# Chunk-output stage: states copied for two groups at once, kernel products ordered by kind, two copies turned into loads

## The chip, the cores and the metric

The kernel runs on one core of a Trainium2 chip. The metric is the time of one execution on the device in microseconds (us). Four such times of the kernel before are known: 2605.39, 2610.87 and 2609.28 us (median 2609.28), and 2605.47 us for the execution that was profiled.

## The reference

A model of two layers over 2048 latent tokens of 1024 channels, with a context of 256 tokens. Layer 0 is windowed attention; the change doesn't touch it. Layer 1 is a bidirectional state-space layer with 64 groups of 16 channels and 64 complex states per group and direction:

```python
for dirn in range(2):
    a_bar = exp(lam * dt)                       # one complex number per group and state
    b_bar = ((a_bar - 1.0) / lam)[..., None] * b_mat
    bu = einsum('gph,blgh->blgp', b_bar, ug)    # ug: inputs of the layer, by group
    xs = diag_scan(a_bar, bu)                   # x[t] = a_bar * x[t-1] + bu[t], started from the context's last state
    y = y + einsum('ghp,blgp->blgh', c_mat, xs).real
y = y + d * ug                                  # then gelu, a GLU and an output projection
```

All inputs and the output are float32.

## The kernel before, in words

The kernel is one program of stages: attention, the input projection of layer 1 (u), chunk states, the scan over chunks, the projection z, the chunk outputs, the GLU, and the output projection. Time is cut into 128 chunks of 16 tokens. For each group, the output of a chunk is the sum of two matrix products: "own" (the chunk's own 256 inputs times a 256 x 256 matrix of kernel values) and "state" (the state that enters the chunk, real and imaginary part, both directions, times a table of powers times C).

The scan leaves the states in one big tile `sall`, as 144 chunk positions x real and imaginary x 64 groups, 128 partitions (64 states of each direction). So the states of one group over the chunks stand 512 bytes apart.

The chunk outputs are made by `phase5` in 16 steps `q` of four groups each. A step's order is written out in a string, for most steps `S0 S1 T2 K T2 G N O0 L O1 L B2 B3` (P5P):

- `S0`, `S1`: for group 0 and 1 of the step `state_part` copies that group's states out of `sall` into a tile `xT` (two activations on ACT, lines 1717 and 1719, one for each direction), and `state_mm` (line 1724) multiplies: `xT` is the stationary operand (the weights), the table `gr` or `gi` the moving one.
- `K`: `ker` makes the kernel values of the next step: for each direction and group a 64-column product (line 1688), for each group a 16-column product with `cb` (line 1693), and one product that adds the skip term to the diagonal (line 1687). They go into one PSUM tile, are copied to `ks` by ACT (line 1697), written to DRAM `qqd` in four pieces (line 1699), and loaded back as the matrices `mq` of the next step's own products (`load_m`, line 1708; two at the end of K, two at the `L`).
- `G`: `gen` makes `gr` and `gi` of the step after the next on POOL (line 1598) and DVE (1599, 1600) from a table tile `tab5`, which `load_tab` (1568) fetches from DRAM `tabd`; the first of their 17 columns is a plain copy of C by ACT (line 1582).
- `N`: `prep` makes the operands `bm` (POOL 1615, DVE 1616 and 1619), `g4` (ACT 1676, from `gr` and `gi`) and `cb` (ACT 1671, a copy out of the table) for the kernel products of the step after the next.
- `O0`, `O1`: own products (line 1735) of groups 0 and 1; `B2`, `B3`: own and state products of groups 2 and 3. A Gelu on ACT (line 1792) follows each group.
- `T2`: two flips back into token order, each of four transposes of 128 x 128 (line 1749) and one copy (line 1753); four flips follow every second step.

Step 0 and the last step have strings of their own (P50, P5L). What stands in the strings is the program's order of writing; a planner then sets the order of each engine's instructions from a simulated timeline, except that the kinds of instructions that `keep` marks (own products, kernel products, and on ACT the copies of lines 1582, 1671, 1676 and 1697) stay in the order of writing. The engines, and the queue of SP, which issues all DMAs of this stage, each work strictly in that planned order.

A float32 matrix product is two passes on TensorE, each with a weight load (PEld) of its own; the profile counts the passes.

Of the kernel before, what the change touches and what calls it, by code (L numbers as in the profile page):

```python
# [6 lines left out]
F32 = mybir.dt.float32  # L7
# [3 lines left out]
AF = mybir.ActivationFunctionType  # L11
# [14 lines left out]
def dap(t, offset, dims):  # L26
    return bass.AP(tensor=t.tensor, offset=t.offset + offset, ap=[list(d) for d in dims])
# [31 lines left out]
WUS = [(2, 'vg'), (1, 'v'), (1, 'v')]  # L59
CS = -2  # L60
RS = 50
MB = 6
ZE = (1, 4, 0)
ZG = 1
ZW = 'vv'
# [21 lines left out]
class Net:  # L87
# [1468 lines left out]
    def phase5(self, uy, sall, es):  # L1556
        nc, a, net = self.nc, self.a, self
        el = ExitStack()
        ps = el.enter_context(self.pool("p5ps", 2, PSUM))
        G, M, pools = {}, {}, []  # L1560
# [4 lines left out]
        def load_tab(q):  # L1565
            sl, hf = divmod(q, 2)
            tab = pools[0].tile([128, 7, 4, 16], F32, name=f"tab5{q % 2}")
            nc.sync.dma_start(tab, self.tabd[sl, :, 2:9].rearrange("p j (g h) -> p j g h", g=8)[:, :, hf * 4:hf * 4 + 4])
            return tab

        def gen(q, tab=None):
            tab = tab or load_tab(q)

            def pw(j):
                return tab[:, 2 + j, :, :, None].to_broadcast([128, 4, 16, 16])

            def cc(j):
                return tab[:, 4 + j, :, None, :].to_broadcast([128, 4, 16, 16])

            gr, gi = (pools[0 if q % 3 == 1 else 2].tile([128, 4, 17, 16], F32, name=f"g{n}{q % 3}") for n in "ri")  # L1580
            for t, j in ((gr, 4), (gi, 5)):
                self.keep("E", nc.scalar.activation(t[:, :, 0], tab[:, j], AF.Copy))
            grw, giw = gr[:, :, 1:17], gi[:, :, 1:17]
            for w, j, k, op in ((grw, 1, 0, OP.add), (giw, 0, 1, OP.subtract)):
                if q < 2:
                    nc.gpsimd.tensor_tensor(w, pw(0), cc(k), op=OP.mult)
                    for h in range(0, 4, 2):
                        hs = slice(h, h + 2)
                        m = ps.tile([128, 4, 128], F32, name="ytp").rearrange("p a b -> p (a b)")
                        m = m.rearrange("p (g t h) -> p g t h", g=2, t=16)  # L1590
                        ins = nc.vector.tensor_mul(m, pw(1)[:, hs], cc(j)[:, hs])
                        if j and h == 0:
                            self.keep("Z", ins)
                        nc.vector.tensor_tensor(w[:, hs], w[:, hs], m, op=op)
                else:
                    m = pools[2].tile([128, 4, 16, 16], F32, name="gm") if j else free[:, 448:1472].rearrange(
                        "p (g t h) -> p g t h", g=4, t=16)
                    nc.gpsimd.tensor_tensor(m, pw(1), cc(j), op=OP.mult)
                    nc.vector.tensor_mul(w, pw(0), cc(k))
                    nc.vector.tensor_tensor(w, w, m, op=op)  # L1600
            G[q] = (gr, gi, tab)
# [4 lines left out]
        def kernel_parts(q, tab, bm, kts, kd, dk):  # L1606
            nc.vector.tensor_mul(kd, self.ident[0:16, None, 0:16].to_broadcast([16, 4, 16]),
                                 dk[:, :, None].to_broadcast([16, 4, 16]))
            mt = ps.tile([128, 2, 256], F32, name="bmt", bufs=1)
            for ri, op in enumerate((OP.subtract, OP.add)):  # L1610
                pr, pi = (tab[:, 6, :, r * 4:r * 4 + 4, None].to_broadcast([128, 4, 4, 16]) for r in range(2))
                br, bi = (tab[:, r, :, None, :].to_broadcast([128, 4, 4, 16]) for r in (ri, 1 - ri))
                kt = kts[ri].rearrange("p (g a) h -> p g a h", a=4)
                m = mt[:, ri].rearrange("p (g a h) -> p g a h", g=4, a=4)
                nc.gpsimd.tensor_tensor(kt, pr, br, op=OP.mult)
                nc.vector.tensor_mul(m, pi, bi)
                for d in range(2):
                    hs = slice(d * 64, (d + 1) * 64)
                    nc.vector.tensor_tensor(bm[ri * 64:(ri + 1) * 64, 1 - d], kt[hs], m[hs], op=op)
# [4 lines left out]
        def first():  # L1624
# [30 lines left out]
            for _ in ker(0):  # L1655
                pass
# [4 lines left out]
        def prep(q):  # L1661
            tab = G[q][2]
            kts = [free[:, c:c + 256].rearrange("p (r h) -> p r h", h=16) for c in (0, 1472)]
            kd = free[0:16, 256 + q % 2 * 64:320 + q % 2 * 64].rearrange("p (g h) -> p g h", h=16)
            bm = pools[1].tile([128, 2, 4, 4, 16], F32, name="bm")
            kernel_parts(q, tab, bm, kts, kd, free[0:16, 384 + q * 4:388 + q * 4])
            g4 = pools[1].tile([128, 2, 4, 64], F32, name="g4")
            cb = pools[1].tile([128, 4, 16], F32, name="cb")
            for ri in range(2):
                rs = slice(ri * 64, (ri + 1) * 64)  # L1670
                self.keep("F", nc.scalar.activation(cb[rs], tab[64:128, 4 + ri], AF.Copy))
                for d in range(2):
                    hs = slice(d * 64, (d + 1) * 64)
                    src = G[q][ri][hs, :, 13 * d:13 * d + 4].rearrange("p g t h -> p g (t h)")
                    if G4E[ri * 2 + d] == "a":
                        self.keep("F", nc.scalar.activation(g4[rs, 1 - d], src, AF.Copy))
                    else:
                        (nc.gpsimd if G4E[ri * 2 + d] == "g" else nc.vector).tensor_copy(g4[rs, 1 - d], src)
            G["ker", q] = bm, g4, cb, kd

        def ker(q):
            bm, g4, cb, kd = G.pop(("ker", q))
            kp = ps.tile([64, 4, 2, 64], F32, name="kps", bufs=1)
            for d in (1, 0):
                for gg in range(4):
                    if d == 0 and gg == 3:
                        nc.tensor.matmul(kp[0:16, :, 1, 0:16], self.ident[0:16, 0:16], kd, start=False, stop=False)
                    ins = nc.tensor.matmul(kp[:, gg, d], bm[:, d, gg].rearrange("p a h -> p (a h)"), g4[:, d, gg],
                                           start=gg == 0 and d == 1, stop=d == 0 and gg == 3)
                    if q:  # L1690
                        self.keep("K", ins)
                    if d == 1:
                        nc.tensor.matmul(kp[0:16, gg, 1, 0:16], bm[:, 0, gg, 3], cb[:, gg], start=False, stop=False)
                    yield
            ks = pools[2].tile([64, 4, 2, 64], F32, name="ks") if q else free[0:64, 896:1408].rearrange(
                "p (g d c) -> p g d c", g=4, d=2)
            self.keep("E", nc.scalar.activation(ks, kp, AF.Copy))
            for i in range(4):
                (nc.scalar if KSQ[i] == "a" else nc.sync).dma_start(
                    dap(self.qqd, q * 4 * 16 * 512 + i * 64, [[2048, 16], [256, 8], [1, 64]]),  # L1700
                    ks[i * 16:(i + 1) * 16].rearrange("p g d c -> p (g d) c"))
            if q:
                load_m(q, 0)
                load_m(q, 1)

        def load_m(q, gg):
            M[q, gg] = pools[1].tile([128, 384], F32, name="mq", bufs=MB)
            nc.sync.dma_start(M[q, gg], dap(self.qqd, q * 4 * 16 * 512 + gg * 512 + 16, [[16, 8], [2048, 16], [1, 384]]))
# [2 lines left out]

        P5 = {}

        def state_part(q, gg):
            g = q * 4 + gg
            xt = pools[1].tile([128, 2, 128], F32, name="xT", bufs=2)
            ins = nc.scalar.activation(xt[0:64], sall[0:64, 15:143, :, g].rearrange("p j r -> p r j"), AF.Copy)
            self.keep("X", ins)
            nc.scalar.activation(xt[64:128], self.rev(sall, 64, 128, 142, 128, g), AF.Copy)
            return xt  # L1720

        def state_mm(q, gg, p, xt, first, kg=None):
            for ri in range(2):
# [33 lines left out]
        def out(q, plan):  # L1757
            sl, hf = divmod(q, 2)
            kg = ker(q + 1) if q < 15 else iter(())
            loads = [2, 3] if q < 15 else []  # L1760
            for tok in plan.split():
                c, n = tok[0], int(tok[1:] or 0)
                if c == "R":
                    prep(1)
# [33 lines left out]
        def early(step):  # L1798
            open_pool()
            if step == 0:  # L1800
                tab1.append(load_tab(1))
            else:
                for gg in range(4):
                    load_m(0, gg)
            if step == ZG:
                gen(1, tab1[0])
# [273 lines left out]
```

## Time and profile before

| what | value |
|---|---|
| median of three runs | 2609.28 us (2605.39 to 2610.87) |
| profiled execution | 2605.47 us, its span 2603.7 us |
| PE busy | 2493.4 us, 96% of the span |
| DVE, ACT, POOL busy | 60%, 44%, 31% |
| mean granted TensorE clock | 0.989 of full speed |
| chunk-output stage | about 1859 to 2057 us of the span |

Busy shares of the whole span are a mean over stages; the stage that the change touches is read from views of that stretch alone. PE stands for matrix products, PEld for their weight loads, SPq for the queue from which SP issues DMAs, "<-" in a name for output and input tiles, and in brackets for what ended the idle time before an instruction.

### The profile page before, as it was taken

The numbers are of one execution on the slowest core, as the hardware profiler recorded it, in microseconds if no ns is written. First come the engines' busy times: TensorE is split into PE (matmuls) and PEld (weight loads), VectorE is DVE, ScalarE is ACT, GpSimd is POOL, SyncE is SP. The second block draws the span as 40 slices with busy tenths as digits, with TensorE's granted clock in tenths as the row PEclk, the third lists the DMA queues.
The fourth block names the chain that finished last, engine by engine and source line by source line (L and its number), as shares of the span: only waits on it lengthen the run. The fifth ranks groups of instructions, "written<-read, shape, count | busy, mean of one in ns | idle before, by whom it ended". The sixth has DMA issues, their size and how long they took to land. (4 is left out here: it accounts for less than half of the span.)

```text
span 2603.7 us, 43687 instructions
## 1 busy us (share of the span) xinstructions
PE 2493.4 (96%) x15838; PEld 2251.8 (86%) x15838; DVE 1555.8 (60%) x3866; ACT 1151.3 (44%) x2651; POOL 817.2 (31%) x701
## 2 busy tenths in 40 slices
PE   7999999998999999999999999899999899999998
PEld 5999989997988999999899988799877688888887
DVE  4773276636898888888732865698576421012454
ACT  3301210136777777777644349611399610001221
POOL 0321331213545455555432222101265222121221
PEclk9999999998999999999999999999999999999999
DMA  8555456477454434434275552376444322223542
GB/s 282 174 166 169 146 168 195 142 192 196 101 139 106 102 91 104 111 93 104 89 202 176 211 158 83 107 237 236 148 100 103 85 81 81 65 81 122 170 140 79
DMA packets 402312, 360.23 MB, mean 138 GB/s; under 512 B 82921, under 2 KB 345129, under 8 KB 402097
## 3 DMA queue, kind: packets, MB, share of 16 engines
q1 hardware_dynamic: 296216, 286.03, 38.3%
q10 hardware_dynamic: 105880, 71.41, 8.6%
q8 instruction: 126, 2.06, 0.3%
q14 instruction: 90, 0.73, 0.1%
HBM read 250.83 MB, written 106.51 MB: 137 GB/s over the span
## 5 line engine op out<-in xcount | busy, mean ns | idle before, releaser
L117 PE MATMUL mm<-hhl,whi 128*128 128x384 f32 x848 | 285.0, 339 | 1.6 <-DVE whi L109 1.6
L118 PE MATMUL mm<-hhl,whi 128*128 128x384 f32 x848 | 285.3, 337 | 0.7 <-POOL hhl L112 0.7
L119 PE MATMUL mm<-hhl,wlo 128*128 128x384 f32 x848 | 284.8, 336 | 0.7 <-DVE wlo L112 0.7
L950 POOL TENSOR_SCALAR P<-P,ri 128x640 f32<-128x640 f32 (+2 forms) x272 | 209.1, 782 | 232.1 <-DVE ri L948 188.1
L969 DVE TENSOR_TENSOR pl<-pt,ph 128x512 fp32r<-128x512 f32 (+1 forms) x384 | 233.6, 608 | 32.6 <-ACT ph L968 29.5
L928 DVE CUSTOM_DVE_ANT_0 P<-S,mask,sink 128x640 f32<-128x640 f32 (+1 forms) x240 | 209.2, 872 | 60.2 <-PE S L919 55.4
L968 ACT ACTIVATE ph<-pt 128x512 fp32r<-128x512 f32 (+1 forms) x384 | 203.0, 529 | 71.2 <-PE pt L964 68.5
L964 PE MATMUL pt<-ident,P 128*128 128x128 f32 x1312 | 213.2, 275 | 12.5 <-DVE pl L969 4.9
L929 ACT ACTIVATE P<-P,nm 128x640 f32<-128x640 f32 (+1 forms) x256 | 208.4, 814 | 25.3 <-DVE nm L928 8.2
L964 PEld LDWEIGHTS pt<-ident,P 128*128 128x128 f32 x1312 | 157.4, 141 | 30.4 <-POOL P L950 10.5
L117 PEld LDWEIGHTS mm<-hhl,whi 128*128 128x128 f32 x848 | 159.3, 189 | 8.4 <-DVE whi L109 2.9
L112 POOL TENSOR_TENSOR wlo<-wraw,whi 128x512 fp32r<-128x512 f32 x60 | 86.6, 1473 | 248.7 <-DVE whi L109 242.2
L118 PEld LDWEIGHTS mm<-hhl,whi 128*128 128x128 f32 x848 | 159.8, 188 | 3.7 <-issue 2.6
L119 PEld LDWEIGHTS mm<-hhl,wlo 128*128 128x128 f32 x848 | 159.8, 188 | 1.9 <-DVE wlo L112 1.0
L117 PE MATMUL zps<-zh,wzh 128*128 128x256 f32 x512 | 146.5, 287 | 7.1 <-DMA zh<-h1d 4.4
L119 PE MATMUL zps<-zh,wzl 128*128 128x256 f32 x512 | 146.0, 286 | 3.3 <-DVE wzl L112 2.0
L118 PE MATMUL zps<-zh,wzh 128*128 128x256 f32 x512 | 145.4, 285 | 0.0
L1907 DVE TENSOR_TENSOR gy<-gps,gs 128x512 f32<-128x512 f32 x32 | 22.1, 691 | 206.0 <-POOL gs L1905 206.0
L1904 ACT ACTIVATE gs<-gps 128x512 f32<-128x512 f32 x32 | 19.1, 598 | 257.2 <-PE gps L119 257.2
L109 DVE CAST whi<-wraw 128x512 fp32r<-128x512 f32 (+1 forms) x80 | 53.6, 720 | 103.2 <-PE mm L118 96.0
L1905 POOL TENSOR_TENSOR gs<-gs,gz 128x512 f32<-128x512 f32 x32 | 43.8, 1367 | 207.6 <-ACT gs L1904 207.6
L117 PEld LDWEIGHTS zps<-zh,wzh 128*128 128x128 f32 x512 | 99.0, 194 | 9.0 <-DMA zh<-h1d 5.1
(560 smaller groups left out, 7524.5 us busy)
## 6 DMA issues: line engine op xcount, KB each, us to landing
zh<-h1d SPq DMA_DIRECT2D x64, 512.0 KB
qta<-qd SPq DMA_DIRECT2D x144, 128.0 KB
qtb<-qd SPq DMA_DIRECT2D x144, 128.0 KB
wraw<-in_w_ada_dram SPq DMA_DIRECT2D x16, 1024.0 KB
wraw<-in_attn_w_in_dram SPq DMA_DIRECT2D x12, 1024.0 KB
mq<-qqd SPq DMA_DIRECT2D x64, 192.0 KB
qd<-oh ACTq DMA_DIRECT2D x48, 192.0 KB
qd<-ol ACTq DMA_DIRECT2D x48, 192.0 KB
```

What stands on the lines that cost most here:

```text
L109: nc.vector.tensor_copy(hi, src)
L112: (nc.gpsimd if lo_eng == "g" else nc.vector).tensor_tensor(lo, src, hi.bitcast(F32), op=OP.subtract)
L117: nc.tensor.matmul(ps, whi(k), mhi(k), start=first and k == 0, stop=False)
L118: nc.tensor.matmul(ps, whi(k), mlo(k), start=False, stop=False)
L119: nc.tensor.matmul(ps, wlo(k), mhi(k), start=False, stop=last and k == nk - 1)
L928: nc.vector.tensor_tensor_reduce(o, sc, mk, -0.125, nsink[:, h:h + 1], OP.add, OP.min, nm)
L929: nc.scalar.activation(p, p, AF.Exp, bias=nm, scale=-1.0, accum_out=SM[i][:, e:e + 1])
L950: (nc.vector if e >= CTXV else nc.gpsimd).tensor_scalar(P[i][e], P[i][e], ri[:, e:e + 1], 1.0, op0=OP.mult, op1=OP.mult)
L964: ins = nc.tensor.transpose(t[:, c - c0], P[i][e][:, k * 128:(k + 1) * 128], self.ident)
L968: nc.scalar.activation(ph[:, c0:c1], t, AF.Copy)
L969: nc.vector.tensor_tensor(pl[:, c0:c1], t, ph[:, c0:c1].bitcast(F32), op=OP.subtract)
L1905: nc.gpsimd.tensor_tensor(sg, sg, z, op=OP.mult)
```

## The change

- `state_part` copies the states of two neighbouring groups at once: the tile `xT` is now 128 x (2, 128, 2), the two groups interleaved, so each pair of activations reads two neighbouring elements at every chunk position and covers two groups. It runs for groups 0 and 2 of a step; the state products of a group take every second element of the tile as weights. There are still two buffers of `xT`, each twice as large; the buffers of `mq` (`MB`) go from 6 to 5.
- In `ker` the products are ordered by kind: the four of direction 1, the four with `cb`, the diagonal one, the four of direction 0. Before, those with `cb` alternated with direction 1.
- The first column of `gr` and `gi`, and `cb`, are loaded from DRAM `tabd` by DMAs from SP. Before, ACT copied them out of the table tile.

```diff
--- before.py
+++ after.py
@@ -59,7 +59,7 @@
 WUS = [(2, 'vg'), (1, 'v'), (1, 'v')]
 CS = -2
 RS = 50
-MB = 6
+MB = 5
 ZE = (1, 4, 0)
 ZG = 1
 ZW = 'vv'
@@ -1578,8 +1578,9 @@
                 return tab[:, 4 + j, :, None, :].to_broadcast([128, 4, 16, 16])
 
             gr, gi = (pools[0 if q % 3 == 1 else 2].tile([128, 4, 17, 16], F32, name=f"g{n}{q % 3}") for n in "ri")
-            for t, j in ((gr, 4), (gi, 5)):
-                self.keep("E", nc.scalar.activation(t[:, :, 0], tab[:, j], AF.Copy))
+            sl, hf = divmod(q, 2)
+            for t, j in ((gr, 6), (gi, 7)):
+                nc.sync.dma_start(t[:, :, 0], self.tabd[sl, :, j].rearrange("p (g h) -> p g h", g=8)[:, hf * 4:hf * 4 + 4])
             grw, giw = gr[:, :, 1:17], gi[:, :, 1:17]
             for w, j, k, op in ((grw, 1, 0, OP.add), (giw, 0, 1, OP.subtract)):
                 if q < 2:
@@ -1668,7 +1669,7 @@
             cb = pools[1].tile([128, 4, 16], F32, name="cb")
             for ri in range(2):
                 rs = slice(ri * 64, (ri + 1) * 64)
-                self.keep("F", nc.scalar.activation(cb[rs], tab[64:128, 4 + ri], AF.Copy))
+                nc.sync.dma_start(cb[rs], self.tabd[q // 2, 64:128, 6 + ri].rearrange("p (g h) -> p g h", g=8)[:, q % 2 * 4:q % 2 * 4 + 4])
                 for d in range(2):
                     hs = slice(d * 64, (d + 1) * 64)
                     src = G[q][ri][hs, :, 13 * d:13 * d + 4].rearrange("p g t h -> p g (t h)")
@@ -1683,15 +1684,18 @@
             kp = ps.tile([64, 4, 2, 64], F32, name="kps", bufs=1)
             for d in (1, 0):
                 for gg in range(4):
-                    if d == 0 and gg == 3:
-                        nc.tensor.matmul(kp[0:16, :, 1, 0:16], self.ident[0:16, 0:16], kd, start=False, stop=False)
                     ins = nc.tensor.matmul(kp[:, gg, d], bm[:, d, gg].rearrange("p a h -> p (a h)"), g4[:, d, gg],
-                                           start=gg == 0 and d == 1, stop=d == 0 and gg == 3)
+                                           start=gg == 0 and d == 1, stop=gg == 3 and d == 0)
                     if q:
                         self.keep("K", ins)
-                    if d == 1:
-                        nc.tensor.matmul(kp[0:16, gg, 1, 0:16], bm[:, 0, gg, 3], cb[:, gg], start=False, stop=False)
                     yield
+                if d == 0:
+                    break
+                for gg in range(4):
+                    ins = nc.tensor.matmul(kp[0:16, gg, 1, 0:16], bm[:, 0, gg, 3], cb[:, gg], start=False, stop=False)
+                    if q and gg == 0:
+                        self.keep("K", ins)
+                nc.tensor.matmul(kp[0:16, :, 1, 0:16], self.ident[0:16, 0:16], kd, start=False, stop=False)
             ks = pools[2].tile([64, 4, 2, 64], F32, name="ks") if q else free[0:64, 896:1408].rearrange(
                 "p (g d c) -> p g d c", g=4, d=2)
             self.keep("E", nc.scalar.activation(ks, kp, AF.Copy))
@@ -1711,13 +1715,19 @@
 
         P5 = {}
 
+        xts = {}
+
         def state_part(q, gg):
-            g = q * 4 + gg
-            xt = pools[1].tile([128, 2, 128], F32, name="xT", bufs=2)
-            ins = nc.scalar.activation(xt[0:64], sall[0:64, 15:143, :, g].rearrange("p j r -> p r j"), AF.Copy)
-            self.keep("X", ins)
-            nc.scalar.activation(xt[64:128], self.rev(sall, 64, 128, 142, 128, g), AF.Copy)
-            return xt
+            if gg % 2 == 0:
+                g = q * 4 + gg
+                x = pools[1].tile([128, 2, 128, 2], F32, name="xT", bufs=2)
+                ins = nc.scalar.activation(x[0:64], sall[0:64, 15:143, :, g:g + 2].rearrange("p j r g -> p r j g"), AF.Copy)
+                self.keep("X", ins)
+                s = sall[64:128]
+                nc.scalar.activation(x[64:128], bass.AP(tensor=s.tensor, offset=s.offset + 142 * 128 + g,
+                                                        ap=[list(s.ap[0]), [64, 2], [-128, 128], [1, 2]]), AF.Copy)
+                xts[0] = x
+            return xts[0][:, :, :, gg % 2]
 
         def state_mm(q, gg, p, xt, first, kg=None):
             for ri in range(2):
```

## Rows read from the trace of the kernel before

**Rows 1.** Busy time by stretches: us, busy us (instructions) of each engine, granted clock, DMA.
```profile
1872.10:1882.00 9.90, 9.83 (x40) 7.21 (x41) 9.24 (x9) 7.28 (x16) 3.67 (x3) 0.51 0.08 11
...
1930.00:1954.00 24.00, 22.13 (x133) 17.28 (x132) 16.78 (x23) 21.82 (x48) 12.57 (x8) 1.00 0.40 98
```

**Rows 2.** Waits from 1857 to 2060 us: us in total, times, longest.
```profile
PEld yp L1724 <- ACT xT L1719: 26.8, 25, 4.8
...
PE yp L1724 <- ACT xT L1719: 16.8, 24, 4.4
```

**Rows 3.** PE's weight loads in order of time: start, us, instruction, passes [idle before].
```profile
1930.75 0.30 PEld L1724 LDWEIGHTS yp<-gr,xT 128*128 128x128 f32 x2 [1.08 <-ACT xT L1719]
...
1933.55 0.19 PEld L1688 LDWEIGHTS kps<-g,bm 128*64 128x64 f32 x2 [0.33 <-DVE gr L1600]
...
1935.16 0.42 PEld L1688 LDWEIGHTS kps<-g,bm 128*64 128x64 f32 x6
...
1935.65 0.10 PEld L1687 LDWEIGHTS kps<-sall,ident 16*16 16x16 f32 x2
...
1936.12 2.46 PEld L1735 LDWEIGHTS yp<-mq,uy 128*128 128x128 f32 x12
...
1938.60 0.41 PEld L1724 LDWEIGHTS yp<-gr,xT 128*128 128x128 f32 x2
...
1947.42 0.86 PEld L1749 LDWEIGHTS ytp<-ident,ysl 128*128 128x128 f32 x8
...
1948.24 2.46 PEld L1735 LDWEIGHTS yp<-mq,uy 128*128 128x128 f32 x12
```

**Rows 4.** Order of time: begin of the second and of the fifteenth kernel products.
```profile
1886.28 0.33 PE L1688 MATMUL kps<-g,bm 128*64 128x64 f32 x2
...
2038.27 0.19 PEld L1688 LDWEIGHTS kps<-g,bm 128*64 128x64 f32 x2 [0.17 <-issue]
```

**Rows 5.** ACT's groups by shape, 1857 to 2060 us: count, busy us, mean ns, idle before.
```profile
L1717 ACT ACTIVATE xT<-sall 64x256 f32<-64x256 f32 x64 | 41.7, 652 | 4.8 <-PE yp L1724 3.4 <-ACT zo L1551 0.4
...
L1676 ACT ACTIVATE g<-gr 64x256 f32<-64x256 f32 x30 | 12.5, 417 | 1.4 <-DVE gr L1594 1.1
...
L1671 ACT ACTIVATE cb<-tab 64x64 f32<-64x64 f32 x30 | 7.7, 256 | 0.5
...
L1582 ACT ACTIVATE gr<-tab 128x64 f32<-128x64 f32 x15 | 3.9, 258 | 0.3
```

**Rows 6.** The same view over the whole span: a copy that reads every 256 bytes.
```profile
L379 ACT ACTIVATE pwe<-pi 64x1024 f32<-64x1024 f32 x1 | 2.0, 2049 | 5.4 <-DVE pwg L382 5.4
```

**Rows 7.** SP's queue in order of time: start, us in which it issued.
```profile
1929.00 2.62 SPq L1708 DMA_DIRECT2D mq<-qqd  x4
1936.85 3.35 SPq L1699 DMA_DIRECT2D qqd<-ks  x4
1940.36 0.47 SPq L1568 DMA_DIRECT2D tab<-tabd  x1
1941.89 2.64 SPq L1708 DMA_DIRECT2D mq<-qqd  x4
```

**Rows 8.** One line's issues: loads in pieces of 64 bytes, ns min/median/max.
```profile
L1395 SPq DMA_DIRECT2D ucs<-ucd x64: 302/447/1437, 1521.3 to 1596.5; - x64
```

**Rows 9.** Order of time in the z stage: two weight loads that follow each other.
```profile
1848.40 0.19 PEld L119 LDWEIGHTS zps<-zh,wzl 128*128 128x128 f32 x1
...
1848.52 0.19 PEld L117 LDWEIGHTS zps<-zh,wzh 128*128 128x128 f32 x1
```

**Rows 10.** Order of time at the stage's start and end.
```profile
1872.17 1.35 PEld L1724 LDWEIGHTS yp<-uy,xT 128*128 128x128 f32 x4 [4.84 <-ACT xT L1719]
...
1885.17 0.87 DVE L1619 TENSOR_TENSOR bm<-sall,bmt 64x256 f32<-64x256 f32 x2
...
2049.94 0.30 PEld L1724 LDWEIGHTS yp<-gr,xT 128*128 128x128 f32 x2 [0.99 <-ACT xT L1719]
```

**Rows 11.** Busy time by stretches: the end of the loads begun at 1941.89.
```profile
1948.70:1949.50 0.80, 0.80 (x6) 0.70 (x5) 0.80 (x1) 0.79 (x3) 0.80 (x2) 1.00 0.00 0
```

## The prediction

> **What bounds the kernel now.** The stage that the change touches is the chunk-output stage, 1859 to 2057 us of the span; I read the busy table by stretches, then the waits of that stretch, then the instructions in order of time, and the rest only for prices.
>
> The table by stretches [rows 1] shows two engines near full in the middle of the stage: of 24 us PE is busy 22.13 and ACT 21.82, DVE 16.78, POOL 12.57. The waits [rows 2] say which of the two is late: weight loads of the state products waited 26.8 us in 25 places, and the products themselves 16.8 us, for the second half of the xT copy (L1719). The order of time [rows 3] shows such a wait, 1.08 us at 1930.75, and that everything else on PE runs back to back. So ACT paces the stage, and PE is close behind.
>
> The stage has 16 steps (one per four channel groups). Its kernel products begin 15 times; the second at 1886.28 and the fifteenth at 2038.27 [rows 4] are 13 periods apart, 151.99 us, so 11.69 us a step.
>
> What PE needs per step if it never waits, from [rows 3]: twelve passes of "own" products from 1936.12 to 1938.60 are 0.207 us each, and the state product behind runs alike (two passes, 0.41 to 0.43 us): 4 groups x 4 products x 2 passes x 0.213 = 6.8 us. The kernel products from 1933.55 to 1936.12: 2.57. Eight transposes from 1947.42 to 1948.24: 0.82, twice in two steps, 0.82 a step. Together 10.2 us; the other 1.5 us of the 11.69 are waits, mostly for xT.
>
> **The change part by part.**
>
> *xT in pairs.* Before, 128 copies of 64 x 256, 0.65 us each, so 16 in two steps, 10.4 us of ACT [rows 5]. After, 64 copies of 64 x 512. Reads of one element in every 512 bytes are dear: 64 contiguous elements take 0.256, 256 contiguous 0.417 [rows 5], so 0.84 ns an element over 0.20 us fixed, while the xT copy's (0.652 - 0.20)/256 is 1.77 ns, and another strided copy of 1024 elements, 2.05 us, gives 1.80 [rows 6]. No row reads two neighbours and then jumps. Ends: 0.20 + 512 x 0.84 ns = 0.63 us, and 0.20 + 512 x 1.77 ns = 1.11 us. Nearest is the present xT copy with the same jump, so I reckon with the dear end: 8 copies in two steps, 8.9 us (cheap end 5.0). Even that is 1.5 us less than before.
>
> [...]
>
> *Two loads by DMA.* ACT loses per two steps 4 cb copies of 0.256 and 4 copies of the first column of gr and gi at 0.25 [rows 5], 2.0 us. ACT's budget for two steps: 21.82 x 23.4/24 = 21.3 now; minus 10.4 and 2.0, plus 8.9, gives 17.8 us of a new 20.4 (13.9 at the cheap end). ACT no longer sets the pace, and since a buffer now holds two groups and there are two, the copy for the first two groups of the next step can start as soon as the second state product of this step has run, a whole half step ahead. The 1.08 us waits should go.
>
> The price of the loads stands on SP: four more issues a step. Nearest rows: the table load, 0.47 us [rows 7], and a load in 64-byte pieces, 0.30 to 1.44, median 0.45 [rows 8]. So 1.8 us a step (1.2 to 5.8) on a queue that is used 3.35 + 0.47 + 2.64 = 6.5 of 11.7 us [rows 7]. Cover: SP is idle from 1931.62 to 1936.85 [rows 7], while the kernel products run, and the buffers are free by then: gr and gi once the last state product of the step before has run, cb once the four cb products have, which now end about 1 us before the kernel products do. Taken: 0 on the path. If the cover goes, they stand between the writes of the kernel tables and the mq loads; what that costs is the first rival.
>
> They add a wait: the ACT copies L1676 read the first column of gr and gi and now wait for a landing. Behind them in ACT's order stand the Gelus and the pair copies. The copies run after the kernel products, some 6 us after the buffer came free, so I take 0; at worst it is the 1.5 us a step that ACT gives back.
>
> *Kernel products by kind.* From 1933.55 to 1935.16 four kernel products alternate with four 16-column cb products, 1.61 us; six kernel passes in a row take 0.49, 0.082 each; the diagonal product 0.21 [rows 3]. After: 16 x 0.082 + 0.21 + the eight cb passes. By estimate these cost between 8 x 0.04 (half a kernel pass: a quarter of the columns, at least) and the present 1.61 - 0.65 = 0.96; I take 0.6 and 0.1 for the changes of kind: 2.2 us, 0.37 less (0 to 0.65).
>
> *Strided weights.* xT is a stationary operand, and its columns now lie 8 bytes apart. No weight load of the trace is strided. At stride one a load is recorded at 0.19 us, yet in the z stage loads and products follow each other every 0.12 us [rows 9], so it hides under a product that has 0.12 itself; here it has 0.213. From below: 0 (nothing becomes faster). From above: the load slows as ACT's strided read does, 1.77/0.84 = 2.1 times, and none of it hides beyond the pass: 0.19 x 2.1 = 0.40 for 0.213, 256 passes x 0.187 = 48 us. If it overlaps as in the z stage, at most 0.12 x 2.1 = 0.25 for 0.213, 10 us. I take 0: the nearest row shows the load hidden, and here it has almost twice the room.
>
> [...]
>
> *MB from 6 to 5.* The four mq loads of a step now reuse buffers freed, at latest, by the third group's own product of the step before. The loads are issued at 1941.89 [rows 7], that product ended by 1938.60 [rows 3]. Cost 0.
>
> **Sum.** New PE need: 6.8 + 2.2 + 0.82 = 9.8. What is late next is small: waits at the kernel products like the 0.33 at 1933.55 [rows 3] and a Gelu now and then, 0.4. So 10.2 a step (9.8 to 10.9): 13 x (11.69 - 10.2) = 19.4 us. DVE needs 16.78/2 = 8.4 a step, POOL 6.3: they fit under 10.2, with the first not by much.
> At the end, the last step's four state products each wait for a single xT copy, 0.99 at 2049.94 the longest [rows 10]; the four keep PE from its pitch for about 2.2 us. Two are prefetched and two come as one pair: 1.9 saved.
> [...] That wait could vanish, but the second kernel products need bm, whose DVE work goes on to 1886 (L1619 at 1885.17 [rows 10]), so whatever PE gains it waits out there: 0.5 (0 to 9).
> Sum 21.8 us. The profiled execution took 2605.47 (span 2603.7), the median of the three is 2609.28; the four together have a mean of 2607.8, from which I count: 2586.0.
>
> **The rivals.**
> 1. *The kernel tables come late.* The loop kernel products -> ks copy -> four writes -> four mq loads -> own products takes from 1936.12 to before 1948.70, when the DMA engines are empty [rows 3, 11], 12.6 us for the last load. At 10.2 a step the last of the four is wanted 10.2 + 2.5 (twelve own passes) + 0.9 (a state product) = 13.6 us after the kernel products end. Slack 1.0; 1.8 us of new issues in between turn it into 0.8 us lost a step: 13 x 0.8 = 10.4 us, 2596.5. For it: loads and tables share one queue. Against: SP has room earlier. 20%.
> 2. *The state products slow down.* Strided weights at 0.30 us a pass would eat 256 x 0.087 = 22 us, all the gain; that is the point from which it decides. At 0.35, between the hidden and the exposed price, 35 us: 2621, slower. Against it the z stage's 0.12 us [rows 9]. 10%.
> 3. *The order doesn't use the pairs.* ACT stays in order; if the planned order puts the pair copy behind a copy that waits for a DMA column, the wait for xT stays, and only the kernel products' 0.37 x 13 = 4.8 remain: 2603. 12%.
> 4. *The start opens too*, the 4.84 us wait and the slow clock go: 8 us more, 2578. 6%.
>
> **How the numbers follow.** Forecast 52%, own range 2577 to 2596. What a measurement of this kernel tells from no change is about 0.2%, 5.2 us. Faster: forecast, rivals 1 and 4, and a third of rival 3: 0.82. Within: two thirds of rival 3 and a tenth of rival 2: 0.09. Slower: the rest of rival 2, 0.09. The range for 8 in 10 takes in rivals 1, 3 and 4 and the near side of rival 2's bounds: 2573 to 2609.
>
> **What would show it.** Right: 64 xT copies of 64 x 512 at 0.63 to 1.11 us; no wait of a state product for xT over 0.5 us in the middle; kernel products done in 2.2 us; period 10.2. Wrong: state products at a pitch over 0.213 us (rival 2); own products that wait for mq (rival 1); L1676 copies or xT waiting on ACT for a DMA (rival 3). The forecast falls if the period stays above 11.

## The result, and the profile after

The changed kernel takes 2589.87 us (median of 4 runs, 2586.34 to 2595.0) against 2610.07 (4 runs); the ratio is 0.9928, 95% interval 0.9906 to 0.9949. Run again beside later experiments it took 2588.85 us against 2608.18, ratio 0.9927 [0.9911, 0.9943]. Forecast were 2586.0. Most of the argument below rests on one trace of each kernel.

The profiled execution took 2591.29 us (span 2589.5), 14.2 less than the profiled one of before. Begin of the second and of the fifteenth kernel products after, in order of time on PE's weight loads (start, us, instruction, passes, idle before and what ended it):

```profile
1886.85 0.93 PEld L1687 LDWEIGHTS kps<-g,bm 128*64 128x64 f32 x8 [8.78 <-issue]
...
2026.58 0.54 PEld L1687 LDWEIGHTS kps<-g,bm 128*64 128x64 f32 x8 [0.17 <-issue]
```

13 periods take 139.73 us, 10.75 a step, against 11.69 [rows 4]: 12.3 us saved. The tail, from the fifteenth kernel products to the end of the last own product, went from 18.89 to 16.26 us: 2.6 saved. The second kernel products start 0.57 us later than before. 12.3 + 2.6 - 0.6 = 14.3 is the whole difference of the two spans. The medians differ by 6 us more, because the profiled execution of before was 4.6 us under its median and that of after 1.4 over. Whether the change brings something ahead of the loop stays open: two profiled executions of the changed kernel, with nearly the same step (10.75 and 10.72), have spans of 2589.5 and 2584.8 us, and they are as far apart before the stage begins (the early kernel products, `kps<-sall`, last begin at 1775.5 and 1770.5); of before there is one trace.

The waits from 1857 to 2060 us, after (us in total, times, longest):

```profile
PEld yp L1745 <- DMA mq<-qqd: 10.8, 15, 1.7
...
PEld yp L1734 <- ACT xT L1727: 0.5, 1, 0.5
...
PE yp L1745 <- DMA mq<-qqd: 5.8, 9, 1.3
```

The 26.8 us of waits for xT [rows 2] are down to 0.5, and own products now wait for mq, which no row of before's answer showed. The busy table of the same 24 us as in [rows 1]:

```profile
1930.00:1954.00 24.00, 22.20 (x137) 17.43 (x138) 22.44 (x25) 14.63 (x31) 14.37 (x9) 1.00 0.52 119
```

ACT fell from 21.82 to 14.63, DVE rose from 16.78 to 22.44, and PE stayed where it was, not full. ACT's groups by shape (count, busy us, mean ns, idle before and what ended it):

```profile
L1724 ACT ACTIVATE xT<-sall 64x512 f32<-64x512 f32 x32 | 21.1, 658 | 1.2 <-ACT zo L1551 0.4
...
L1677 ACT ACTIVATE g<-gr 64x256 f32<-64x256 f32 x30 | 12.5, 416 | 40.4 <-DMA gr<-tabd 24.5 <-DVE bmt L1617 6.9 <-DVE bm L1620 4.2
```

A copy of a pair costs 658 ns, what a copy of one group cost (652, [rows 5]). One step of PE after:

```profile
1927.91 0.54 PEld L1687 LDWEIGHTS kps<-g,bm 128*64 128x64 f32 x8 [0.32 <-issue]
1928.52 0.26 PEld L1695 LDWEIGHTS kps<-cb,bm 128*16 128x16 f32 x8
1928.81 0.11 PEld L1698 LDWEIGHTS kps<-sall,ident 16*16 16x16 f32 x2
1929.02 0.54 PEld L1687 LDWEIGHTS kps<-g,bm 128*64 128x64 f32 x8
1930.93 0.73 PEld L1745 LDWEIGHTS yp<-mq,uy 128*128 128x128 f32 x4 [1.36 <-DMA mq<-qqd]
1931.97 0.73 PEld L1745 LDWEIGHTS yp<-mq,uy 128*128 128x128 f32 x4 [0.31 <-DMA mq<-qqd]
1933.16 0.73 PEld L1745 LDWEIGHTS yp<-mq,uy 128*128 128x128 f32 x4 [0.47 <-issue]
1933.92 0.41 PEld L1734 LDWEIGHTS yp<-gr,xT 128*128 128x128 f32 x2
```

The kernel products run in 1.65 us, from 1927.91 to 1929.56, and take 1.72 from their begin to that of the next product where that doesn't wait (2.57 in [rows 3], counted so); state products keep their 0.41 to 0.43 us a pair of passes although their weights lie 8 bytes apart; and the own products, twelve in a row in [rows 3], come in fours as each mq lands. Why it lands late stands in SP's order of time (start, us in which it issued):

```profile
1925.99 2.62 SPq L1712 DMA_DIRECT2D mq<-qqd  x4
1928.67 0.80 SPq L1583 DMA_DIRECT2D gr<-tabd  x1
1929.51 0.51 SPq L1583 DMA_DIRECT2D gi<-tabd  x1
1930.06 1.16 SPq L1672 DMA_DIRECT2D cb<-tabd  x2
1931.32 3.54 SPq L1703 DMA_DIRECT2D qqd<-ks  x4
1935.80 0.36 SPq L1568 DMA_DIRECT2D tab<-tabd  x1
1938.33 2.62 SPq L1712 DMA_DIRECT2D mq<-qqd  x4
```

The idle stretch that the prediction counted on has shrunk. From the end of the mq loads to the time when ks is there it was 5.2 us in [rows 7] (1931.62 to 1936.85); here it is 1.8 (1928.61 to 1930.38). The four new loads begin right behind the mq loads, while the kernel products run, and hold SP for 2.55 us, where 1.8 were reckoned. So the writes of the tables (qqd), which could start when ks is there at 1930.38, start at 1931.32. From the end of the kernel products to the last mq issue, mean of eleven steps (the fourth to the fourteenth kernel products; the parts are ks copied, wait of qqd, issue of qqd, up to the first mq, issue of mq):

```
before  0.76 + 0.03 + 2.73 + 1.70 + 2.64 = 7.86 us
after   0.73 + 0.59 + 3.35 + 2.28 + 2.64 = 9.59 us
```

And this is DVE and POOL in the same step:

```profile
1930.57 1.21 DVE L1601 TENSOR_TENSOR gi<-gi,sall 128x1024 f32<-128x1024 f32 x1
1931.70 1.94 DVE L1608 TENSOR_TENSOR sall<-ident,sall 16x64 f32<-16x64 f32 x1
...
1930.72 2.84 POOL L1599 TENSOR_TENSOR gm<-tab 128x1024 f32<-128x1024 f32 x1 [3.43 <-DVE gr L1601]
1933.53 1.92 POOL L1599 TENSOR_TENSOR sall<-tab 128x1024 f32<-128x1024 f32 x1
```

The small product kd (16 x 64, L1608; the operand of the diagonal product), 0.20 to 0.21 us where no POOL product runs, takes 1.94 and ends at 1933.64, right behind gm (1933.56), POOL's first product in `gen`. Its mean over 13 is 1.81 us. In the trace of before it was 0.61; there it mostly waited for the kernel products first, and came when gm was over or nearly so (here begun at 1933.26, 2.85 us long):

```profile
1935.97 0.21 DVE L1607 TENSOR_TENSOR sall<-ident,sall 16x64 f32<-16x64 f32 x1 [1.65 <-PE kps L1687]
...
1933.26 2.85 POOL L1598 TENSOR_TENSOR gm<-tab 128x1024 f32<-128x1024 f32 x1 [5.20 <-DVE gr L1600]
```

### The profile page after: what moved, and what is told of

Read it like the earlier page. It is cut to its first block, busy times and chain, and to the rows that moved or that the text cites. A ratio compares the mean times of both kernels' runs of the same rounds, so it can differ in the third digit from the quotient of the medians.

```text
span 2589.5 us, 43615 instructions
## 1 busy us (share of the span) xinstructions
PE 2476.6 (96%) x15838; PEld 2246.0 (87%) x15838; DVE 1570.4 (61%) x3866; ACT 1093.7 (42%) x2527; POOL 810.0 (31%) x701
```

## The experiments

Two theories were held for the step of 10.75 us where 10.2 were forecast: the loads make mq late, or DVE, slowed beside POOL, is the next bound. First the three parts alone and the change without its loads, then kd on POOL with and without the loads, then the places of loads on the queues. All ratios are to the kernel before, run on the same chip beside it; they are the recorded ones, and lie up to 0.0011 above the quotient of the two medians.

| kernel | median us | ratio, 95% | step us |
|---|---|---|---|
| before | 2607.6 to 2610.1 | | 11.69 |
| e4_loads: loads alone | 2602.86 | 0.9986 [0.9976, 0.9997] | 11.64 |
| e3_kind: by kind alone | 2598.43 | 0.9973 [0.9962, 0.9983] | 11.22 |
| e2_pairs: pairs alone | 2590.78 | 0.9946 [0.9932, 0.9959] | 10.77 |
| whole change, twice | 2589.87, 2588.85 | 0.9928, 0.9927 | 10.75, 10.72 |
| e1_act_copies: without the loads | 2585.76 | 0.9926 [0.9913, 0.9938] | 10.41 |
| e5_kd_pool: e1, kd on POOL | 2578.47 | 0.9894 [0.9878, 0.9910] | 9.97 |
| e6_after_kd_pool: whole, kd on POOL | 2587.07 | 0.9929 [0.9916, 0.9943] | 10.55 |
| e9_act_queue: e6, loads on ACT's queue | 2586.65 | 0.9920 [0.9904, 0.9937] | 10.29 |
| e10_pairs_kd_pool: e2, kd on POOL | 2591.33 | 0.9939 [0.9920, 0.9957] | 10.74 |
| e7_tab_late: e1, tab behind mq | 2595.64 | 0.9961 [0.9946, 0.9976] | 11.46 |
| e8_both: e7, kd on POOL | 2590.07 | 0.9937 [0.9923, 0.9951] | 11.02 |

Where each step's time lies on PE is worked out from the begins of all its products between the third and the fifteenth kernel products: the time from one product to the next, summed by kind, us a step. These are 12 steps; the period before them, in which the stage gets going, is in the 13 of the column above, so the two differ (e2: 10.53 and 10.77). A wait is booked under the product ahead of it: if the first own product waits for mq, that stands under the kernel products. The last column is the way from the end of the kernel products to the last mq issue. e7 and e8 are left out, as records are missing from their traces.

```
               kernel products  transposes   own   state | to last mq
before              2.57          0.95      3.51   4.78  |   7.86
e4_loads            2.57          0.95      3.58   4.68  |   7.80
e3_kind             1.77          0.95      3.51   4.92  |   8.02
e2_pairs            2.57          0.95      3.51   3.50  |   7.91
e10_pairs_kd_pool   2.57          0.95      3.51   3.50  |   8.11
after               1.84          0.99      4.22   3.59  |   9.59
e1_act_copies       1.94          0.95      3.79   3.50  |   8.76
e6_after_kd_pool    1.74          0.95      4.17   3.55  |   9.26
e9_act_queue        1.72          0.95      3.92   3.50  |   8.72
e5_kd_pool          1.72          0.95      3.56   3.50  |   8.02
```

The least of each column is what PE needs: 1.72 + 0.95 + 3.51 + 3.50 = 9.68 us; what lies above it is waiting.

**The change without its loads (e1_act_copies).**

```diff
-            for t, j in ((gr, 6), (gi, 7)):
-                nc.sync.dma_start(t[:, :, 0], self.tabd[sl, :, j]...)
+            for t, j in ((gr, 4), (gi, 5)):
+                self.keep("E", nc.scalar.activation(t[:, :, 0], tab[:, j], AF.Copy))
...
-                nc.sync.dma_start(cb[rs], self.tabd[q // 2, 64:128, 6 + ri]...)
+                self.keep("F", nc.scalar.activation(cb[rs], tab[64:128, 4 + ri], AF.Copy))
```

> The changed kernel with one part undone: the first column of gr and gi, and cb, are copied by ACT again instead of loaded by SP. In the changed kernel the step period is 10.75 us, of which PE waits about 0.9 for mq. Theory: the four loads stand on SP between the ks copy and the qqd writes (start of the writes 1 to 1.5 us after the copy's end, before the change 0.03), so the mq loads come late. Then the writes start at once, PE's waits for mq go, the period falls to 10.0 to 10.4, and the kernel is 5 to 10 us faster than the changed one, 24 to 30 below the kernel before. Rival A: ACT needs the 1.0 us a step; then waits for xT or Gelu come back and the time is that of the changed kernel or up to 10 us more. Rival B: the loop over the tables is too long in any case; then period and time stay within 2 us of the changed kernel.

The step fell by 0.34 us, 4.4 us in 13, under the 5 to 10 us expected of the loads, and the writes start at once, but the time is 22 us below before, not 24 to 30, and its ratio can't be told from the whole change's. Own products still wait for mq, 0.28 us a step among themselves and 0.22 right behind the kernel products, as here:

```profile
1933.35 0.73 PEld L1744 LDWEIGHTS yp<-mq,uy 128*128 128x128 f32 x4 [0.79 <-DMA mq<-qqd]
```

DVE is now the fullest engine but PE, in the order of the page (PE, PEld, DVE, ACT, POOL; 127 us of the loop), and its products follow each other almost without a gap (kd begins at 1924.20, 1934.57 and 1944.93):

```profile
1899.00:2026.00 127.00, 123.76 (x839) 104.09 (x838) 117.24 (x130) 103.78 (x236) 69.12 (x44) 1.00 0.42 108
```

So the loads cost something, but taking them away uncovers a second bound close behind.

**Pairs alone (e2_pairs)**: the change's `state_part` and MB, the old order of kernel products and ACT's copies.

```diff
-MB = 6
+MB = 5
...
-            xt = pools[1].tile([128, 2, 128], F32, name="xT", bufs=2)
+            if gg % 2 == 0:
+                x = pools[1].tile([128, 2, 128, 2], F32, name="xT", bufs=2)
```

> The kernel before with the pair copies alone (and MB 5). Theory that ACT's xT copies paced the stage and the pairs are what gives the gain: period 10.4 to 10.8 (PE needs 10.2 with the old kernel products), 12 to 18 us below the kernel before. Rival: the gain came from the kernel products by kind (1.65 us instead of 2.57); then only 3 to 6 us are left here.

The step is 10.77, that of the whole change, and PE has no gap at all in 127 us:

```profile
1899.00:2026.00 127.00, 127.00 (x802) 107.51 (x802) 111.22 (x127) 99.40 (x229) 68.54 (x44) 1.00 0.42 102
```

As expected: the pairs alone make PE the bound, with state products at 3.50 us a step instead of 4.78. All the rest of the change adds nothing to the step that this had not brought.

**By kind alone (e3_kind)**: the order of `ker`, with single xT copies.

```diff
-                    if d == 1:
-                        nc.tensor.matmul(kp[0:16, gg, 1, 0:16], bm[:, 0, gg, 3], cb[:, gg], ...)
                     yield
+                for gg in range(4):
+                    ins = nc.tensor.matmul(kp[0:16, gg, 1, 0:16], bm[:, 0, gg, 3], cb[:, gg], ...)
```

> The kernel before with the kernel products by kind alone. Theory that ACT paces the stage: PE saves 0.9 us a step and waits that much longer for xT; 0 to 4 us below the kernel before. Rival, PE paces: 0.9 x 13 = 12 us below.

The gain lies between the two expectations (0 to 4 us, and 12): 9.4 us between the medians and 0.47 us a step, so neither holds. Kernel products fall by 0.80 us a step, and in the twelve steps of the table only 0.13 of it goes into longer waits for xT. Weight loads still wait for xT as long as before (1857 to 2060 us):

```profile
PEld yp L1727 <- ACT xT L1722: 27.6, 25, 4.5
```

That ACT paces and PE still gains is no contradiction, as ACT had waited for PE. ACT's waits for PE from 1899 to 2026 us, two lines of before and the one of e3:

```profile
ACT ks L1697 <- PE kps L1688: 5.5, 5, 1.1
ACT xT L1717 <- PE yp L1724: 2.8, 6, 0.5
...
ACT ks L1700 <- PE kps L1686: 1.6, 6, 0.3
```

In these 127 us ACT was busy 115.69 before and is 121.88 in e3.

**Loads alone (e4_loads)**

```diff
-                self.keep("E", nc.scalar.activation(t[:, :, 0], tab[:, j], AF.Copy))
+                nc.sync.dma_start(t[:, :, 0], self.tabd[sl, :, j]...)
```

> The kernel before with the loads by DMA alone. Theory that ACT paces the stage: ACT is freed of 1.0 us a step, up to 13 us below the kernel before, less what the late tables and ACT's waits for gr cost: 3 to 10 below. Rival: the loads cost more than the copies, because ACT stands still until gr has landed (in the changed kernel 24.5 us in 9 places); then the kernel is 0 to 10 us slower than before.

ACT loses 2.0 us in two steps, and the step 0.05. Waits for xT stay (24.3 us), and a part of what ACT gained it waits for the columns:

```profile
PEld yp L1725 <- ACT xT L1720: 24.3, 25, 4.4
...
ACT g L1677 <- DMA gr<-tabd: 9.1, 6, 2.8
```

The time, 5 us lower between the medians, is in the expected range, but the loop makes only 0.6 us of it; the second kernel products begin 3.1 us earlier, 2.0 of which are there before the stage begins. So it doesn't show the theory. In a step of 11.6 us the loads find the idle stretch on SP: the way to the last mq is 7.80 us. What was argued for them holds there; it fails where the step is shorter.

**kd on POOL, without the loads (e5_kd_pool)**

```diff
-            nc.vector.tensor_mul(kd, ident..., dk...)
+            (nc.gpsimd if q else nc.vector).tensor_tensor(kd, ident..., dk..., op=OP.mult)
```

> Pairs and products by kind, ScalarE's copies kept, and the gated start states of the later chunks (kd) multiplied by GpSimd instead of VectorE. Theory (VectorE's loop with GpSimd now sets the step: the kd product takes 1.94 us because it runs into a GpSimd product and ends with it): without it VectorE is left with some 8.4 to 8.6 us of work a step, the step falls from 10.41 us to 9.7 to 10.1, and the time lies 4 to 8 us under the same kernel with kd on VectorE. Rival (the late loads of mq set it): the step stays within 0.15 us of 10.41, the time within 2 us. [...]

The theory's numbers: step 9.97, 7.3 us under e1. PE is full:

```profile
1899.00:2026.00 127.00, 126.88 (x854) 109.12 (x851) 108.87 (x116) 104.26 (x239) 77.59 (x55) 1.00 0.44 113
```

DVE's 1.94 us became 0.58 on POOL, and the way to mq shortened from 8.76 to 8.02 us: the gap ahead of mq, in which SP's load of tab waits for tab's readers on DVE and POOL, fell from 2.93 to 2.20. So DVE's lateness had reached PE through mq: tab can be loaded only when the readers of its buffer are done, and mq stands behind it on SP. SP's waits for DVE ahead of the load of tab, 1899 to 2026 us, e1 and then e5:

```profile
SPq L1568 <- DVE bmt L1616: 22.2, 10, 2.9
...
SPq L1568 <- DVE bmt L1616: 4.8, 7, 1.5
```

The two theories are thus two causes of one wait. But the stretching moved to the next product: bmt takes 1486 ns where it took 837 in e1 (lines of DVE and of POOL, 1899 to 2010 us):

```profile
L1616 DVE TENSOR_TENSOR bmt<-tab 128x256 f32<-128x256 f32 x22 | 32.7, 1486 | 0.8
...
L1607 POOL TENSOR_TENSOR sall<-ident,sall 16x64 f32<-16x64 f32 x11 | 6.4, 584 | 14.3 <-PE kps L1697 14.3
```

**kd on POOL with the whole change (e6_after_kd_pool)**: the same edit.

> The whole change, with kd on GpSimd. Theory (VectorE's loop sets the step of 10.75 us, and the loads behind one another on SP come next, close under it): the step falls to 10.2 to 10.6, the time 2 to 6 us under the whole change. Rival (the late loads set the step): the step stays at 10.7 to 10.8, the time within 2 us, and TensorE's waits for mq (10.8 us of weight loads) grow.

The step fell by 0.2 us only, within the 10.2 to 10.6 expected; in the time nothing can be told from the whole change. Against e5, measured beside it, this is the price of the loads once DVE is out of the way: 0.58 us a step, 7.6 us in 13, and ratios 0.9929 and 0.9894 whose intervals don't meet. The table puts it at one place: own products 4.17 against 3.56.

**tab behind the mq loads (e7_tab_late), and with kd on POOL (e8_both).** The load of the tables, the last thing ahead of mq on SP, is written behind the last two mq loads of a step, and both kinds of loads are kept in the order of writing:

```diff
-            nc.sync.dma_start(tab, ...)
+            self.keep("E", nc.sync.dma_start(tab, ...))
...
-            nc.sync.dma_start(M[q, gg], ...)
+            self.keep("E", nc.sync.dma_start(M[q, gg], ...))
...
+                    if not loads and q + 4 < 16:
+                        tabs[q + 4] = load_tab(q + 4)
```

> Pairs and products by kind with ScalarE's copies, and the load of the tables (tab) issued behind the loads of mq instead of ahead of them, so that no mq load stands behind it on SP. Theory (VectorE's loop sets the step): TensorE's weight loads wait less for mq (7.0 us over 15 waits falls under 3), and the step stays within 0.15 us of 10.41. Rival (the late mq sets it): the step falls to 9.9 to 10.1, and the time 4 to 7 us.

> Both edits together: kd on GpSimd and the tables' load behind mq's, with ScalarE's copies. Theory: with VectorE's loop relieved the late mq would be the next bound, and with both gone TensorE's own work (9.3 to 9.8 us) is; the step falls to 9.5 to 9.9, the time to 2575 to 2580 us against 2608 before. Rival (GpSimd or VectorE still binds): the step stays at 10.2 or more and the time is within 2 us of the kernel with kd on GpSimd alone.

No expectation of either came out as a whole (e8's rival has the step, 10.2 or more, but its time is 11.6 us over e5's, not within 2). Waits for mq halve, from 7.0 to 3.5 us, but the tables now come too late for POOL, and the step grows to 11.46 and 11.02. e7's waits from 1886 to 2030 us:

```profile
POOL gm L1598 <- DMA tab<-tabd: 32.7, 7, 8.1
...
PE kps L1686 <- DVE bm L1619: 6.1, 5, 3.9
```

The edit thus doesn't say what an earlier mq alone would bring; it shows that tab can't go behind it either. SP's queue has two loads that each want to be first.

**The loads on ACT's queue (e9_act_queue)**

```diff
-                nc.sync.dma_start(t[:, :, 0], self.tabd[sl, :, j]...)
+                nc.scalar.dma_start(t[:, :, 0], self.tabd[sl, :, j]...)
...
-                nc.sync.dma_start(cb[rs], ...)
+                nc.scalar.dma_start(cb[rs], ...)
```

> The whole change with kd on GpSimd, and the four small loads of a step (gr, gi, cb twice) issued by ScalarE's queue instead of SP's. Theory (the loads cost 0.58 us a step, 10.55 against 9.97 us, because of where they stand on SP: behind the mq loads that release them late, and ahead of the qqd stores): the step falls to 10.0 to 10.2, the time to 2578 to 2583 us against 2608 before, as with ScalarE's copies. Rival (a load of 64-byte runs lands too late for ScalarE's copies of g wherever it is issued, or its issue stops ScalarE): the step stays at 10.4 to 10.7 and the time at 2585 to 2590.

In between: step 10.29, where 10.0 to 10.2 and 10.4 to 10.7 had been expected, and the time like e6's. The wait of qqd for its place on SP is gone (0.03 us), and so are most of ACT's waits for a landing (0.6 us for gr's column and 2.2 for gi's, where after has 24.5):

```profile
L1677 ACT ACTIVATE g<-gr 64x256 f32<-64x256 f32 x30 | 12.5, 416 | 5.4 <-DVE gr L1595 3.0 <-DVE gr L1601 0.8 <-DMA gr<-tabd 0.6
```

So the place on SP makes about half of the 0.58 us. The other half goes with a longer issue of qqd (2.95 us, e5 2.52) and a later mq (2.41, e5 2.20); that the loads take the DMA engines' time meanwhile fits this, but was not tried by itself. Own products also wait 3.1 us in five places for ACT's Gelu (ysl), of which e5 shows none in the same stretch (1857 to 2060 us); whether the issues on ACT delay the Gelu was not tried.

**Pairs alone, kd on POOL (e10_pairs_kd_pool)**: e5's edit on e2.

> Pairs alone (kernel products in the old order, 2.64 us, and ScalarE's copies), with kd on GpSimd. Theory (with the pairs alone TensorE's own work sets the step of 10.77 us; VectorE's loop becomes a bound only when the products by kind have shortened it): no change, step 10.65 to 10.8, time within 2 us of pairs alone (17 us under before). Rival (VectorE's loop bounds pairs alone already): the step falls by 0.3 us or more, to 10.45 or less, and the time by 4 us or more.

No change, as the theory had it: 10.74, every PE column of the table the same. DVE's slow kd costs nothing as long as PE needs 10.5 us a step. It is a bound only behind the gain of the order by kind.

**The whole change again (after2)**

> The whole change again, beside the other two, for a comparison with the version with ScalarE's copies and with kd on GpSimd: 2587 to 2591 us against 2608, a step of 10.7 to 10.8 us by every theory.

2588.85 us, step 10.72: the table's rows of after nearly come out again (own 4.08, state 3.62).

## Why the prediction was right, and where it wasn't

The time (2589.87, forecast 2586.0, own range 2577 to 2596) and the main mechanism were right. The forecast's sum of 21.8 us stands against 14.2 between the two profiles and 19 to 20 between the medians (19 by either ratio). That the time came out within 4 us is in part luck: the loop, which was to bring 19.4, brought 12.3, and some 5 to 6 us between the medians are in neither of the two traces. Step by step:

- *"ACT paces the stage, and PE is close behind."* The pairs alone bring the loop to PE's need (e2), so the bound was read rightly. But ACT waited for PE in its turn, and a shorter PE alone already brings 0.47 us a step (e3).
- *Pairs.* Reckoned at the dear end, 1.11 us; measured 0.658, close to the cheap end, 0.63. It made no odds, since ACT was out of the way by either. 512 elements in pairs take what 256 single ones took (658 and 652 ns). The waits for xT went as forecast.
- *Strided weights.* 0 taken, 0 measured: state products take 3.50 us a step for 16 passes, 0.219 each, as the own products with plain weights do (3.51). Rival 2 is out. So is a price of MB 5: e2 and e5 have it and run at PE's need.
- *Kernel products.* The term was mis-sized: 0.37 us taken, 0 to 0.65 allowed, 0.85 measured (2.57 to 1.72). It was worked out from the time of passes, but what the new order removes is changes of kind: ten before (cb and the diagonal between 64-column products), three after. 0.85 / 7 = 0.12 us for each on average, by estimate. With this the need of PE is 9.68, where 9.8 was forecast; own and state products (7.01 against 6.8) and transposes (0.95 against 0.82) were reckoned a little low.
- *Two loads, "0 on the path"*: the step that failed. SP's idle stretch [rows 7] belonged to a step of 11.69 us. In the shorter step the mq loads before them release them later, so that they stand ahead of qqd, and rival 1 came in part: own products wait 0.71 us a step (4.22 against 3.51), and 0.11 more right behind the kernel products. That this is near the rival's 0.8 is chance: 0.50 of these waits are still there without the loads (e1). With kd out of DVE's way (e5, e6) the loads cost 0.58. That they free ACT was worth 0.05 alone, and nothing behind the pairs. Their landing wait on ACT came (24.5 us, 3.9 the longest) and cost nothing seen on PE.
- *DVE "fits under 10.2, the first not by much"*: it didn't fit. The 8.4 us a step were taken from a trace in which kd mostly came when gm was over or nearly so. In e1, without the loads, DVE's products repeat every 10.4 us with hardly a gap, and the step is 10.41; with kd on POOL it is 9.97. PE feels it as a late mq, by way of the load of tab.
- *Small waits 0.4*: measured 10.65 - 9.68 = 0.97 in the twelve steps of the table, most of it for mq.
- *Start 0.5, tail 1.9*: -0.6 and 2.6. No run shows the start's 0.5, which stood for the wait of 4.84 us at 1872 [rows 10]; measured, the second kernel products begin 0.57 us later. As forecast, PE waits at the second kernel products for bm instead (8.78 us above; the DVE chain runs from 1873.89 to then without a gap). The wait of 4.84 us is down to 1.70, and the slow clock behind it is gone (granted clock 0.99 from 1872.1 to 1882, where [rows 1] has 0.51). But after the 8.78 us in which PE stood still the granted clock was 0.50, from 1886.8 to 1890; the wait and the slow stretch have moved.

Two errors offset each other in part: kernel products brought 0.5 us a step more, and the waits were 0.6 more than forecast. What was left over put the step at 10.75, inside the stated 9.8 to 10.9. Rival 3 is out with the waits for xT, and the gain of rival 4 at the start didn't come.

The version that follows is e5, pairs and order by kind, ACT's copies kept, kd on POOL: 2578.47 us, ratio 0.9894 [0.9878, 0.9910], under both kernels. Its loop is at what PE needs (9.73 against 9.68 in the table).

## What to carry to other kernels

When a step gets shorter, an idle stretch on a queue or an engine must be measured anew against the new step: ask what releases each instruction and what it will then stand ahead of. A part that frees an engine behind the bound is worth nothing there and can still cost (here 0.34 to 0.58 us a step). A busy sum taken from one trace is no need: the small product kd grew ninefold, from 0.21 to 1.94 us, when it came beside POOL's gm.

## What the runs showed of the hardware

- Beside a running POOL product some of DVE's products took longer. kd, with both operands in SBUF, took 0.20 to 0.21 us with no POOL product beside it, and 1.94 where it began 0.98 us behind gm; it ended 0.08 us after gm (1933.64 and 1933.56, above). bmt, also from two SBUF operands, took 0.43 us begun with none beside it (1889.90 in the trace of before) and 1.20 begun beside one (1934.54 after); its mean was 837 ns in e1 and 1486 in e5. The reverse shows too: gm, begun 0.15 us behind gi on DVE, takes 2.84 us, while the like product that follows takes 1.92. bm, with one operand in PSUM, kept its 0.42 us: 0.85 for two with no POOL product beside them (1889.01 before) and with one (1933.65 after). What makes the others longer was not tried.
- Changing between kinds of kernel products on PE (64 columns, 16 columns, the diagonal) cost 0.12 us each time on average, by estimate (2.57 to 1.72 us with the same products in another order, seven changes fewer); by kind it is paid three times a step instead of ten. What in a change costs the time was not tried.
- Weights with a stride of two elements cost nothing here: their load is recorded at 0.196 us (contiguous 0.189 to 0.190), and a pass takes 0.219 us either way.
